# RWKV-7 stage of a four-mixer decoder trunk: key blocks first, state in two half-head chains, outputs and LayerNorm with dims on partitions

## The chip, the cores and the metric

One core of a Trainium2 chip runs the whole kernel. The metric is the device time of one execution in microseconds, as the median of several runs.

## The reference, cut to what matters

Four layers, each `h = h + Mixer(RMSNorm(h))` and `h = h + SqReLU_MLP(RMSNorm(h))`, on x of (1, 256, 1024) float32; the mixers are S5, mLSTM, FoX and RWKV-7 in that order. The change touches RWKV-7 alone (16 heads of 64):

```python
xr, xw, xk, xv, xa, xg = (x + dx * mu[idx] for idx in range(6))   # dx = x_prev - x
r, k, v = xr @ W_r, xk @ W_k, xv @ W_v
w_log = -softplus(-(w0 + tanh(xw @ W_w) @ w_up)) - 0.5;  decay = exp(-exp(w_log))
a = sigmoid(a0 + (xa @ W_a) @ a_up);  g = sigmoid(xg @ W_g) @ g_up
kk = heads(k * k_k), normed per head;  k_mod = k * (1 + (a - 1) * k_a)
def step(state, inp):
    sa = einsum('bhij,bhj->bhi', state, -kk_t)
    state = state * w_t + sa (x) (kk_t * a_t) + v_t (x) k_t      # (x): outer product
    return state, einsum('bhij,bhj->bhi', state, r_t)
y = head_layer_norm(y) * ln_g + ln_b + sum(r * k_mod * r_k) * v
out = (y * g) @ w_out
```

## The kernel before, in words

The stages run one after another: s5, mlp0, mlstm, mlp1, fox, mlp2, rwkv, mlp3, final. Activations of the RWKV stage are kept turned, with 128 of the 1024 dims on partitions and the 256 time steps in columns, as eight tiles, taken in four blocks b of two tiles (four heads). Half hf is blocks 2hf and 2hf+1. The recurrence is taken in four chunks c of 64 steps: within a chunk it is a triangular system, between chunks a state of 64x64 per head is carried.

- *Head* (L1383 to L1402): the reciprocal norm of each row is spread over partitions by a matmul (`rstd_row`, L372), h is transposed, and VectorE scales it (xn, L1392). `mix` (L1402) is eight VectorE multiply-adds that make one of the six mixed inputs into one of the two halves of xm.
- *main* (L1792): the small projections wl and al, then for each b `k_part` and `r_part`, then `v_part` for each b, then gl. A block's projection (`projN`, L422) is 16 float32 matmuls, 32 instructions, into one of two PSUM banks with the tag pa; weights come through SyncE's queue into three buffers w.
- *k_part* (L1427): pw and pq (L1436, L1437), tanh, the scan of the decay over a chunk (L1448), exponentials, then after k the squares, and in `rest` pn (L1480: the block matrix bones times the squares), Ln and Exp (L1483, L1484) and five VectorE steps (L1486 to L1491) into X and bk. Its temporaries hold the tags s, hi, lo, two buffers each; `rest` ends with the last use of hi and lo.
- *inner* (L1541), one per half: products of bk (weights) and X, both its a half (64 columns) and its r half (64 columns) in one matmul of 128 columns (L1553), masks, a regrouping through memory (L1578, L1581: ScalarE's queue writes, then reads), a 15-step loop on VectorE (L1599, L1601), a second round trip (L1605, L1608), and the block solve z, dx, dy (L1634 to L1666). The PSUM banks are acc0 to acc3.
- *over* (L1674): the four chunks one behind another, both halves together: b1, rh, b3, sv, b4, scaled state, and the outputs in b2 (L1686 to L1716), with time steps on partitions. `norm` (L1720) takes bn_stats per head, a Pool power, and 8 ScalarE scalings a chunk (L1734).
- *gate* (L1742): the gate's projection (L1752, L1753). *outp* (L1758): transposes py (L1768), 8 ScalarE scalings by ln_g and ln_b (L1776), two VectorE steps, the split in two fp32r parts, then the output projection: each of the eight weight blocks times both parts, 12 matmuls of 512 columns (L442; in `tail` L474).

Order: these are generators, run by `Order` (L143). It takes the next name of a hand-written list (`SEQ["rwkv"]`, L211) that can go; with the list used up, of the tasks whose inputs are ready by `Clock`'s own costs the one with the lowest priority number (the third argument of `spawn`), then the oldest. A task waits at `yield event`; `od.fire` sets an event. What is written earlier has priority; on an engine a later instruction can stand ahead of an earlier one that has to wait for operands or buffers.

Of the kernel before, what the change touches and what calls it, by code (L numbers as in the profile page):

```python
# [8 lines left out]
F32 = mybir.dt.float32  # L9
# [9 lines left out]
KT = 8  # L19
# [123 lines left out]
class Order:  # L143
# [22 lines left out]
    def run(self):  # L166
# [44 lines left out]
    "rwkv": (  # L211
# [1140 lines left out]
def rwkv(K):  # L1352
# [9 lines left out]
    with ExitStack() as st:  # L1362
# [22 lines left out]
        rb = K.rstd_row(K.rstd())  # L1385
        for kp in range(KT // 2):
            if kp % 2 == 0:
                xts = K.turned(kp // 2)
            p = xts[kp % 2]
            n, k0 = kp // 2, 2 * (kp % 2)  # L1390
            for j in range(2):
                nc.vector.scalar_tensor_tensor(out=xn[n][:, k0 + j], in0=p[:, j * T:(j + 1) * T],  # L1392
                                               scalar=col("rw_norm_g", 2 * kp + j), in1=rb, op0=ALU.mult, op1=ALU.mult)
            x = xn[n][:, k0:k0 + 2]
            nc.scalar.mul(dx[n][:, k0:k0 + 2, :1], x[:, :, :1], -1.0)
            nc.vector.tensor_tensor(out=dx[n][:, k0:k0 + 2, 1:], in0=x[:, :, :T - 1], in1=x[:, :, 1:], op=ALU.subtract)
        xm = K.xtp.tile([128, 2, KT, T], F32, name="xm", tag="xhl")

        def mix(n, dst):

            for k in range(KT):
                nc.vector.scalar_tensor_tensor(out=xm[:, dst, k], in0=dx[k // 4][:, k % 4], scalar=col("rw_mu", n * KT + k),  # L1402
                                               in1=xn[k // 4][:, k % 4], op0=ALU.mult, op1=ALU.add)
            return xm[:, dst]

# [9 lines left out]
        ready = [Event(), Event()]  # L1415
        v_ev = [Event() for _ in range(4)]
        t_ev, f_ev = [Event(), Event()], Event()
        y_ev = Event()
        g_ev = Event()
        yn, rbm, Yt = [None] * 2, [None] * 2, [None] * 2  # L1420
        C = -0.5 * float(np.exp(-0.5))
        tmp, kks = {}, []
        q4 = lambda n, t, bufs=2: one.tile(SHAPE4, F32, name=n, tag=t, bufs=bufs)
        bank = lambda n, k: K.pacc.tile([128, 512], F32, name=n, tag=f"acc{k}")
        u3 = lambda t: t.rearrange("p a c t -> p (a c) t")

        def k_part(b, xk):  # L1427
# [22 lines left out]
            E1 = dbl.tile([128, 2, 4, 65], F32, name="E1", tag="E1")  # L1450
# [6 lines left out]
            yield GO  # L1457
            out = []
            yield from K.projN(two(i["rw_k"], b), xk, out)
            pk = out[0]  # L1460
# [16 lines left out]
            def rest():  # L1477
# [10 lines left out]
                for e in range(2):  # L1488
                    nc.vector.scalar_tensor_tensor(out=X[hf][R[e], e, ps0, :, :64], in0=kr[R[e]], scalar=-1.0,
                                                   in1=E1[R[e], :, :, :64], op0=ALU.mult, op1=ALU.mult)  # L1490
                    nc.vector.scalar_tensor_tensor(out=bk[b][R[e], :, :, e], in0=tha[R[e]], scalar=0.5, in1=E2[R[e]],  # L1491
                                                   op0=ALU.mult, op1=ALU.mult)
                yield GO
            tmp["kk", b] = od.spawn(f"k{b}", rest())
            kks.append(tmp["kk", b])

        def r_part(b, xr):
# [11 lines left out]
            if b % 2:  # L1509
                od.fire(ready[hf])  # L1510
# [29 lines left out]

        def inner(hf):  # L1541

            yield ready[hf]
            for ev in kks[2 * hf:2 * hf + 2]:
                yield ev
            x = X[hf]
            ar = q4("araw", "ar")
            rb_ = rbm[hf] = q4("rb", "rb")
            for p in range(4):
                ms = [bank(f"m{hf}", 2 * (p % 2) + e).rearrange("p (c t) -> p c t", c=4) for e in range(2)]  # L1550
                for c in range(4):
                    for e in range(2):
                        nc.tensor.matmul(ms[e][:, c], bk[2 * hf + p // 2][R[e], p % 2, c].rearrange("p a t -> p (a t)"),  # L1553
                                         x[R[e], e, p, c], start=True, stop=True)
                for e in range(2):
                    m = ms[e]
                    kr, br = R[1 - e], R[e]
                    nc.scalar.copy(out=ar[br, p], in_=m[br, :, :64])
                    nc.vector.tensor_tensor(out=x[kr, e, p], in0=m[kr], in1=mask[kr].unsqueeze(1).broadcast_to([64, 4, 128]),
                                            op=ALU.mult)  # L1560
                    nc.scalar.copy(out=rb_[br, p], in_=m[br, :, 64:])
                yield WAIT if p % 2 else GO
            for e in range(2):
                nc.gpsimd.affine_select(out=u3(rb_)[R[e]], in_=u3(rb_)[R[e]], pattern=[[0, 16], [1, 64]],
                                        compare_op=ALU.is_ge, fill=0.0, base=0, channel_multiplier=-1)
# [16 lines left out]

            for b in (2 * hf, 2 * hf + 1):
                bkT[b] = one.tile([128, 2, 2, 4, 64], F32, name="bkT", tag="bk", bufs=5)
                for p in range(2):
                    t = bank(f"bt{hf}", 2 * hf + p).rearrange("p (c e t) -> p c e t", c=4, e=2)
                    for c in range(4):
                        nc.tensor.transpose(t[:, c].rearrange("p e t -> p (e t)"),
                                            bk[b][:, p, c].rearrange("p a t -> p (a t)"), K.ident)
                    nc.scalar.copy(out=bkT[b][:, :, p].rearrange("p e c t -> p c e t"), in_=t)  # L1590
                    yield GO
# [36 lines left out]
            for g in range(2):  # L1628
                us = slice(8 * g, 8 * g + 8)
                au = aus[g]  # L1630
                z = bank(f"z{hf}", 2 * hf).rearrange("p (u t) -> p u t", u=8)
# [6 lines left out]
                dx_ = bank(f"dx{hf}", 2 * hf + 1).rearrange("p (u t) -> p u t", u=8)  # L1638
                dy = bank(f"dy{hf}", 2 * hf).rearrange("p (u t) -> p u t", u=8)
# [11 lines left out]
            z = bank(f"z2{hf}", 2 * hf).rearrange("p (u t) -> p u t", u=16)  # L1651
# [10 lines left out]
            dy = bank(f"dy2{hf}", 2 * hf + 1).rearrange("p (u t) -> p u t", u=16)  # L1662
# [11 lines left out]
        def over():  # L1674

            for ev in t_ev + v_ev:
                yield ev
            pairs = [(hf, p, e) for hf in range(2) for p in range(4) for e in range(2)]
            for hf in range(2):
                yn[hf] = q4("yn", "ar")  # L1680
            sc = None
            bk8 = lambda n, k: bank(n, k).rearrange("p (a b) -> p a b", a=8)
            for c in range(4):
                b1, b2 = bk8("b1", 0), bk8("b2", 2 + c % 2)
                for hf, p, e in pairs:
                    nc.tensor.matmul(b1[R[e], 4 * hf + p], X[hf][:, e, p, c, :64], sv[:, hf, e, p, c], start=True, stop=True)  # L1686
                rh = K.ev.tile([128, 8, 64], F32, name="rh", tag="lo")
                nc.scalar.copy(out=rh, in_=b1)
                for hf, p, e in pairs:
                    nc.tensor.matmul(b2[R[e], 4 * hf + p], X[hf][:, e, p, c, 64:], sv[:, hf, e, p, c], start=(hf + p == 0), stop=False)  # L1690
                yield WAIT
                b3 = bk8("b3", 1)
                for hf, p, e in pairs:
                    nc.tensor.matmul(b3[R[e], 4 * hf + p], Yt[hf][R[e], p, c], rh[R[e], 4 * hf + p], start=True, stop=True)
                s8 = lambda e, c: sv[R[e], :, e, :, c, :]
                b8 = lambda t: t.rearrange("p (h a) t -> p h a t", h=2)
                nc.scalar.copy(out=s8(0, c), in_=b8(b3[R[0]]))
                nc.vector.tensor_copy(out=s8(1, c), in_=b8(b3[R[1]]))
                yield WAIT
                if c < 3:  # L1700
                    b4 = bk8("b4", 0)
                    for hf, p, e in pairs:
                        nc.tensor.matmul(b4[R[e], 4 * hf + p], bkT[2 * hf + p // 2][:, e, p % 2, c], sv[:, hf, e, p, c], start=True, stop=True)
                    eb = eL[:, :, c].unsqueeze(2).broadcast_to([128, 8, 64])
                    sn = K.ev.tile([128, 8, 64], F32, name="sc", tag="s")
                    src = b4
                    if sc is not None:
                        nc.vector.tensor_tensor(out=sc, in0=sc, in1=b4, op=ALU.add)
                        src = sc
                    for e in range(2):  # L1710
                        nc.vector.tensor_tensor(out=s8(e, c + 1), in0=b8(src[R[e]]), in1=b8(eb[R[e]]), op=ALU.mult)
                    if c < 2:
                        nc.vector.tensor_tensor(out=sn, in0=src, in1=eb, op=ALU.mult)
# [289 lines left out]
```

## Time and profile before

| | us |
|---|---|
| median of 3 runs (lowest to highest) | 1406.84 (1398.44 to 1409.97) |
| profiled execution | 1410.3 |
| its span, first to last instruction | 1408.6 |
| TensorE busy / VectorE / ScalarE | 1323.0 / 873.0 / 716.1 |
| mean granted TensorE clock | 0.966 |

The profile lists each instruction of one execution. A matmul's row lasts until its modelled end, which overlaps the next one's, so what one costs in a stream is the distance from start to start. A busy share near 100% at a clock below 1 is not full work: the granted clock says how fast TensorE was allowed to run. PE is TensorE's matmuls, PEld its weight loads, DVE VectorE, ACT ScalarE, ACTq ScalarE's DMA issue.

### The profile page before, as it was taken

How to read it: one execution, taken by the hardware profiler on the slowest of the kernel's cores; microseconds unless marked ns; L12 is line 12 of the kernel's file. 1: busy time of each engine (PE TensorE's matmuls, PEld its weight loads, DVE VectorE, ACT ScalarE, POOL GpSimd, SP SyncE). 2: the span in 40 equal slices, each digit the busy share in tenths (PEclk: the TensorE clock that was granted, in tenths of full speed). 3: DMA queues.
4: the chain of work that ended last, by engine and by line, in shares of the span. 5: the costliest groups of instructions: out<-in, count | busy, mean ns of one | idle time of the engine just before them, and what ended most of it. 6: DMA issues, size and time to landing. Idle time of an engine off the chain costs nothing.

```text
span 1408.6 us, 23397 instructions
## 1 busy us (share of the span) xinstructions
PE 1323.0 (94%) x9492; PEld 1155.8 (82%) x9492; DVE 873.0 (62%) x1431; ACT 716.1 (51%) x1188; POOL 41.8 (3%) x64
## 2 busy tenths in 40 slices
PE   4799999999999999999999999998998888899997
PEld 3667989998988999889888999986777675799996
DVE  8985555568786555575866555556686443555554
ACT  7945454457645544464554644442544346454443
POOL 3000000001010000000100000000000010000000
PEclk9699999999999999999999999999999996899998
DMA  4045555564535655556334555552333211355553
GB/s 176 16 132 181 166 184 192 183 200 157 184 131 166 193 183 191 187 168 245 123 119 163 181 193 182 192 183 78 117 113 96 78 51 44 113 191 191 190 184 120
DMA packets 71532, 216.14 MB, mean 153 GB/s; under 512 B 19132, under 2 KB 19732, under 8 KB 70912
## 3 DMA queue, kind: packets, MB, share of 16 engines
q1 hardware_dynamic: 56880, 206.30, 44.5%
q10 hardware_dynamic: 14496, 8.24, 2.1%
q8 instruction: 74, 1.21, 0.4%
q14 instruction: 34, 0.28, 0.1%
q0 software_dynamic: 48, 0.11, 0.0%
HBM read 211.71 MB, written 2.91 MB: 152 GB/s over the span
## 4 chain that ended last, share of the span: by engine, by line
PE 60%; issue 18%; DVE 12%; DMA 5%; ACT 4%; POOL 1%; ACTq 0%; POOLq 0%; SPq 0%; DVEq 0%
PE acc L442 21%; PE pa L383 8%; PE pa L384 8%; PE pa L385 8%; PE pa L422 5%; DVE wl L288 2%; PE g L442 1%; ACT wh L287 1%; PE acc L474 1%; PE pa L406 1%; PE pa L408 1%; DVE pd L1599 1%; PE pa L407 1%; DMA w<-in_fox_qk 1%; DVE t L627 1%
## 5 line engine op out<-in xcount | busy, mean ns | idle before, releaser
L288 DVE TENSOR_TENSOR wl<-w,wh 128x1024 fp32r<-128x1024 f32 x350 | 430.4, 1231 | 374.1 <-ACT wh L287 373.3
L287 ACT ACTIVATE wh<-w 128x1024 fp32r<-128x1024 f32 x350 | 370.3, 1059 | 448.0 <-PE pa L384 148.4
L385 PE MATMUL pa<-xhl,wl 128*128 128x256 f32 x1264 | 358.1, 283 | 2.0 <-DVE wl L288 2.0
L383 PE MATMUL pa<-xhl,wh 128*128 128x256 f32 x1264 | 359.4, 284 | 0.0
L384 PE MATMUL pa<-xhl,wh 128*128 128x256 f32 x1264 | 358.1, 283 | 0.0
L383 PEld LDWEIGHTS pa<-xhl,wh 128*128 128x128 f32 x1264 | 242.1, 192 | 4.5 <-issue 1.2
L384 PEld LDWEIGHTS pa<-xhl,wh 128*128 128x128 f32 x1264 | 242.2, 192 | 2.9 <-issue 0.5
L385 PEld LDWEIGHTS pa<-xhl,wl 128*128 128x128 f32 x1264 | 242.2, 192 | 2.6 <-DVE wl L288 2.6
L442 PE MATMUL acc<-wh,hi 128*128 128x512 f32 x552 | 172.8, 394 | 2.6 <-ACT hi L287 1.8
L442 PE MATMUL acc<-wl,hi 128*128 128x512 f32 x552 | 171.4, 392 | 0.0
L442 PE MATMUL acc<-wh,lo 128*128 128x512 f32 x552 | 170.9, 391 | 0.1
L442 PEld LDWEIGHTS acc<-wl,hi 128*128 128x128 f32 x552 | 104.2, 189 | 22.6
L442 PEld LDWEIGHTS acc<-wh,lo 128*128 128x128 f32 x552 | 104.1, 189 | 22.7 <-DVE lo L288 0.5
L422 PE MATMUL pa<-xm,w 128*128 128x256 f32 x448 | 112.2, 403 | 4.8 <-DVE xm L1402 4.8
L442 PEld LDWEIGHTS acc<-wh,hi 128*128 128x128 f32 x552 | 99.6, 190 | 20.6 <-ACT hi L287 2.1
L422 PEld LDWEIGHTS pa<-xm,w 128*128 128x128 f32 x448 | 86.3, 200 | 21.0 <-DVE xm L1402 5.5
L288 DVE TENSOR_TENSOR lo<-s,hi 128x512 fp32r<-128x512 f32 x64 | 43.9, 685 | 1.4 <-ACT hi L287 1.4
L507 DVE SCALAR_TENSOR_TENSOR s<-pa,r 128x512 f32<-128x512 f32 x64 | 43.8, 684 | 0.0
L287 ACT ACTIVATE hi<-s 128x512 fp32r<-128x512 f32 x64 | 39.5, 617 | 5.3 <-DVE s L507 5.3
L505 ACT ACTIVATE r<-pa 128x512 f32<-128x512 f32 x64 | 37.1, 580 | 0.0
L442 PE MATMUL acc<-wh,xhl 128*128 128x512 f32 x128 | 34.9, 391 | 0.0
L353 ACT ACTIVATE xhl<-xt,vecs 128x256 fp32r<-128x256 f32 x48 | 21.0, 472 | 22.4 <-PE xt L338 20.3
(392 smaller groups left out, 1572.2 us busy)
## 6 DMA issues: line engine op xcount, KB each, us to landing
w<-in_mlp_up SPq DMA_DIRECT2D x128, 512.0 KB, 3.5
w<-in_mlp_dn SPq DMA_DIRECT2D x128, 512.0 KB, 3.5
w<-in_s_w_glu SPq DMA_DIRECT2D x16, 512.0 KB, 4.2
w<-in_fox_qk SPq DMA_DIRECT2D x16, 512.0 KB, 4.0
w<-in_ml_qk SPq DMA_DIRECT2D x8, 512.0 KB, 3.8
w<-in_ml_v SPq DMA_DIRECT2D x8, 512.0 KB, 3.5
w<-in_ml_o SPq DMA_DIRECT2D x8, 512.0 KB, 3.4
w<-in_ml_out SPq DMA_DIRECT2D x8, 512.0 KB, 3.4
```

The costliest lines, as they stand in the source:

```text
L287: self.nc.scalar.activation(out=hi, in_=src, func=AF.Copy)
L288: self.nc.vector.tensor_tensor(out=lo, in0=src, in1=hi.bitcast(F32), op=ALU.subtract)
L353: nc.scalar.activation(out=xhl[:, k, 0, :], in_=s, func=AF.Identity, scale=g)
L383: nc.tensor.matmul(out, wh[:, ks], xhl[:, k, 0, :], start=(k == 0), stop=False)
L384: nc.tensor.matmul(out, wh[:, ks], xhl[:, k, 1, :], start=False, stop=False)
L385: nc.tensor.matmul(out, wl[:, ks], xhl[:, k, 0, :], start=False, stop=(k == KT - 1))
L406: nc.tensor.matmul(o, wh[:, ks], xhl[:, k, 0, :], start=(k == 0 and f == 0), stop=False)
L407: nc.tensor.matmul(o, wh[:, ks], xhl[:, k, 1, :], start=False, stop=False)
L422: nc.tensor.matmul(p[:, f * T:(f + 1) * T], w[:, k * 128:(k + 1) * 128], x[:, k], start=(k == 0), stop=(k == KT - 1))
L442: nc.tensor.matmul(acc[tt * 2 + n], a[:, ts], w[:, n * 512:(n + 1) * 512], start=s0, stop=s1)
L505: nc.scalar.activation(out=r, in_=p, func=AF.Relu)
L507: nc.vector.scalar_tensor_tensor(out=s, in0=p, scalar=0.0, in1=r, op0=ALU.max, op1=ALU.mult)
```

## The change

The list `SEQ["rwkv"]` is taken out, so the order comes from priorities and `Clock`. Rows of h are scaled by the reciprocal norm before they are transposed, and the first mix is made pair by pair. `main` runs k0 to k3, then r0 to r3, then v0 to v3, then gl; the second gate weights come on SyncE's queue into w buffers. `inner` starts on kks and multiplies X's first half; `rmul` does X's second half after r. `over` and `norm` run once per half; the output matmul has its operands exchanged, so that y has dims on partitions in banks acc1 and acc3 (half 0) or pa (half 1). LayerNorm is two matmuls with block matrices (cen takes off the mean, bones sums the squares), Ln and Exp; ln_g and ln_b are folded into the gate and into bv.

```diff
+        rr = K.rstd()
+        hn = [[K.ev.tile([128, 512], F32, name="hn", tag=("r", "hi")[n]) for tt in range(2)] for n in range(2)]
+            nc.scalar.activation(out=hn[n][0], in_=K.h[0][:, hs], func=AF.Copy, scale=rr[:, 0:1])
+            nc.vector.tensor_scalar(out=hn[n][1], in0=K.h[1][:, hs], scalar1=rr[:, 1:2], scalar2=None, op0=ALU.mult)
...
+                nc.scalar.activation(out=xn[n][:, k0 + j], in_=p[:, j * T:(j + 1) * T], func=AF.Copy,
+                                     scale=col("rw_norm_g", 2 * kp + j))
...
+            mix(1, 0, (2 * kp, 2 * kp + 1))
...
+        def products(b, ms, ts):
+            for p in range(2):
+                for c in range(4):
+                    for e in range(2):
+                        nc.tensor.matmul(ms[e][:, p, c], bk[b][R[e], p, c].rearrange("p a t -> p (a t)"),
+                                         x[R[e], e, p0 + p, c, ts], start=True, stop=True)
+            for e in range(2):
+                nc.vector.tensor_tensor(out=x[kr, e, p0:p0 + 2, :, ts], in0=ms[e][kr],
...
+        def rmul(b):
+            yield r_ev[b]
+            yield kks[b]
+            ms = products(b, [K.ps("mr", "ps") for e in range(2)], slice(64, 128))
...
         def inner(hf):
-            yield ready[hf]
+            for b in (2 * hf, 2 * hf + 1):
+                yield kks[b]
+                ms = products(b, [bank(f"m{hf}", 2 * (b % 2) + e) for e in range(2)], slice(0, 64))
...
-                dx_ = bank(f"dx{hf}", 2 * hf + 1).rearrange("p (u t) -> p u t", u=8)
-                dy = bank(f"dy{hf}", 2 * hf).rearrange("p (u t) -> p u t", u=8)
+                dx_ = bank(f"dx{hf}", 3).rearrange("p (u t) -> p u t", u=8)
+                dy = bank(f"dy{hf}", 2).rearrange("p (u t) -> p u t", u=8)
...
-        def over():
-            for ev in t_ev + v_ev:
+        def over(hf):
+            for ev in (t_ev[hf], *v_ev[2 * hf:2 * hf + 2], *rms[2 * hf:2 * hf + 2]):
                 yield ev
+            if hf:
+                yield g_ev
+            w = bank(f"ov{hf}", 2 * hf).rearrange("p (g a t) -> p g a t", g=2, a=4)
+                yp[2 * hf + j] = K.pp.tile([128, 512], F32, name="pa", tag="pa", bufs=2) if hf else bank("y", 1 + 2 * j)
...
+                    nc.tensor.matmul(y4[p // 2][R[e], p % 2, c], sv[:, hf, e, p, c], X[hf][:, e, p, c, 64:],
+                                     start=(c == 0 and p % 2 == 0), stop=False)
...
+        def norm(hf):
+            yield gate_ev
+            if hf:
+                yield n_ev[0]
+            for b in bs:
+                nc.scalar.copy(out=yb, in_=yp[b])
+                nc.tensor.matmul(pc[b], cen, yb, start=True, stop=True)
+                nc.scalar.activation(out=sq[b], in_=pc[b], func=AF.Square, scale=0.125)
+            for b in bs:
+                nc.tensor.matmul(pv, bones, sq[b], start=True, stop=True)
+                nc.scalar.activation(out=rs[b], in_=pv, func=AF.Ln, bias=eps)
+            for b in bs:
+                nc.scalar.activation(out=rs[b], in_=rs[b], func=AF.Exp, scale=-0.5)
+            for b in bs:
+                nc.vector.tensor_tensor(out=u, in0=pc[b], in1=rs[b], op=ALU.mult)
+                nc.vector.tensor_tensor(out=u, in0=u, in1=gates[b].rearrange("p a t -> p (a t)"), op=ALU.mult)
+                nc.vector.tensor_tensor(out=u, in0=u, in1=bv[b].rearrange("p a t -> p (a t)"), op=ALU.add)
+                od.fire(u_ev[b])
...
         def outp(b):
-            yield y_ev
-            yield gate_ev
+            yield u_ev[b]
...
         def main():
+            yield from K.projN(two(i["rw_k"], 0), xk, out)
+            for b in range(4):
+                k_part(b, out[b])
+                yield GO
+                if b < 3:
+                    yield from K.projN(two(i["rw_k"], b + 1), xk, out)
+                    yield kks[b]
+            for b in range(4):
                 yield from r_part(b, xr)
...
+            for n in range(2):
+                gup.append(K.wraw.tile([128, D], F32, name="w", tag="w"))
+                nc.sync.dma_start(out=gup[n][:rows], in_=i["rw_g_up"][128 * n:128 * n + rows])
...
+        rms = [od.spawn(f"r{b}", rmul(b), 1) for b in range(4)]
+        for hf in range(2):
+            od.spawn(f"c{hf}", over(hf), 0)
```

## Rows read from the trace of the kernel before

**Rows 1.** Busy time by stretch of the RWKV stage, in us.

```profile
core 0: us, PE busy (x) PEld busy (x) DVE busy (x) ACT busy (x) POOL busy (x), PEclk, DMA share, GB/s
949.00:970.40 21.40, 14.45 (x62) 10.88 (x60) 18.65 (x48) 3.36 (x13) 2.07 (x5) 0.84 0.13 36
970.40:1058.00 87.60, 85.86 (x444) 69.91 (x444) 61.18 (x126) 41.61 (x82) 2.52 (x4) 0.98 0.36 117
1058.00:1126.00 68.00, 57.99 (x823) 45.95 (x823) 34.50 (x68) 28.78 (x60) 2.93 (x4) 0.90 0.34 90
1126.00:1162.40 36.40, 31.81 (x637) 25.54 (x633) 18.33 (x73) 15.59 (x41) 4.92 (x3) 1.00 0.17 51
1162.40:1181.70 19.30, 14.59 (x34) 7.25 (x33) 3.52 (x21) 10.61 (x26) 1.64 (x1) 0.50 0.00 0
1200.30:1217.30 17.00, 10.30 (x40) 7.98 (x38) 6.87 (x11) 7.30 (x14) 0.00 (x0) 0.70 0.18 63
```

**Rows 2.** TensorE in order of time: start, us, operation, count, idle before.

```profile
958.95 9.92 PE L422 MATMUL pa<-xm,w 128*128 128x256 f32 x32 [4.80 <-DVE xm L1402]
...
970.38 14.08 PE L422 MATMUL pa<-xm,w 128*128 128x256 f32 x64
984.30 1.02 PE L1480 MATMUL pn<-sq,cst 128*128 128x512 f32 x2
...
1005.41 1.13 PE L1437 MATMUL pq<-tw,up 64*128 64x256 f32 x4
1006.47 1.13 PE L422 MATMUL pa<-xm,w 128*128 128x256 f32 x4
1007.53 1.16 PE L1553 MATMUL m<-X,bk 64*128 64x128 f32 x16
1008.62 1.13 PE L422 MATMUL pa<-xm,w 128*128 128x256 f32 x4
...
1129.93 1.15 PE L1694 MATMUL b<-rh,Y 64*64 64x64 f32 x32
...
1139.97 0.70 PE L422 MATMUL pa<-xm,w 128*128 128x256 f32 x2
...
1199.38 0.62 PE L442 MATMUL acc<-wl,hi 128*128 128x512 f32 x2
1199.84 0.62 PE L442 MATMUL acc<-wh,lo 128*128 128x512 f32 x2
```

**Rows 3.** Groups by line and form, 948 to 1217 us, TensorE and ScalarE.

```profile
L422 PE MATMUL pa<-xm,w 128*128 128x256 f32 x448 | 112.2, 403 | 4.8 <-DVE xm L1402 4.8
L1553 PE MATMUL m<-X,bk 64*128 64x128 f32 x128 | 10.5, 290 | 4.2 <-ACT rb L1561 4.2
L1776 ACT ACTIVATE y<-py,vecs 64x128 f32<-64x128 f32 x32 | 14.5, 454 | 0.9 <-PE py L1768 0.5
```

**Rows 4.** VectorE and ScalarE in order of time: mixes, then the key chain.

```profile
959.41 12.35 DVE L1402 SCALAR_TENSOR_TENSOR xm<-dx,vecs,xn 128x256 f32<-128x256 f32 x31
...
995.54 1.27 DVE L1448 TENSOR_TENSOR_SCAN L<-reset,ld 128x256 f32<-128x256 f32 x2
...
1004.51 1.28 ACT L1483 ACT_TABLE_LOAD   x1
...
1005.81 0.63 ACT L1483 ACTIVATE rn<-rn 128x512 f32<-128x512 f32 x1
...
1008.77 0.69 DVE L1486 TENSOR_TENSOR kr<-kr,rn 128x512 f32<-128x512 f32 x1 [3.82 <-ACT rn L1484]
...
1014.07 1.25 DVE L1448 TENSOR_TENSOR_SCAN L<-reset,ld 128x256 f32<-128x256 f32 x2
...
1039.35 1.26 DVE L1448 TENSOR_TENSOR_SCAN L<-reset,ld 128x256 f32<-128x256 f32 x2
```

**Rows 5.** The chain of waits, 1056 to 1084 us: start, us, what.

```profile
1058.80 5.18 DMA rw_y<-yx
```

**Rows 6.** Transfers of the page: KB of one, us from issue to landing.

```profile
w<-in_mlp_dn SPq DMA_DIRECT2D x128, 512.0 KB, 3.5
```

More of the change, by code (lines that the diff above doesn't have):

```diff
@@ L1384, in rwkv, with mix @@
         dx = [K.whl.tile([128, 4, T], F32, name=f"dx{n}", tag="wl") for n in range(2)]
[L1385 to L1396, printed above, removed]
         xm = K.xtp.tile([128, 2, KT, T], F32, name="xm", tag="xhl")
-        def mix(n, dst):
-            for k in range(KT):
+        def mix(n, dst, ks=range(KT)):
+            for k in ks:
                 nc.vector.scalar_tensor_tensor(out=xm[:, dst, k], in0=dx[k // 4][:, k % 4], scalar=col("rw_mu", n * KT + k),
@@ L1681, in over @@
             sc = None
-            bk8 = lambda n, k: bank(n, k).rearrange("p (a b) -> p a b", a=8)
             for c in range(4):
[L1684 to L1687, printed above, removed]
+                b1, b3 = w[:, 0], w[:, 1]
+                for p, e in pairs:
+                    nc.tensor.matmul(b1[R[e], p], X[hf][:, e, p, c, :64], sv[:, hf, e, p, c], start=True, stop=True)
@@ L1693, in over @@
[L1693 to L1698, printed above, removed]
+                for p, e in pairs:
+                    nc.tensor.matmul(b3[R[e], p], Yt[hf][R[e], p, c], rh[R[e], p], start=True, stop=True)
@@ L1699, in over @@
+                nc.scalar.copy(out=s4(0, c), in_=b3[R[0]])
+                nc.vector.tensor_copy(out=s4(1, c), in_=b3[R[1]])
                 yield WAIT
                 if c < 3:
[L1701 to L1705, printed above, removed]
@@ L1706, in over @@
-                    src = b4
+                    for p, e in pairs:
+                        nc.tensor.matmul(b1[R[e], p], bkT[2 * hf + p // 2][:, e, p % 2, c], sv[:, hf, e, p, c], start=True, stop=True)
+                    eb = eL[:, 4 * hf:4 * hf + 4, c].unsqueeze(2).broadcast_to([128, 4, 64])
+                    src = b1
                     if sc is not None:
-                        nc.vector.tensor_tensor(out=sc, in0=sc, in1=b4, op=ALU.add)
+                        nc.vector.tensor_tensor(out=sc, in0=sc, in1=b1, op=ALU.add)
@@ L1717, in over @@
[L1717 removed]
+                for p, e in pairs:
+                    nc.tensor.matmul(y4[p // 2][R[e], p % 2, c], sv[R[e], hf, e, p, c], rbm[hf][R[e], p, c],
+                                     start=False, stop=(c == 3 and p % 2 == 1))
                 yield WAIT
[L1720 to L1737 removed]
@@ new lines, in gate @@
+                    nc.tensor.matmul(pg[:, js], gup[0][:, fs], sg[0], start=True, stop=False)
+                    nc.tensor.matmul(pg[:, js], gup[1][:32, fs], sg[1], start=False, stop=True)
+                for j in range(2):
+                    js = slice(j * T, (j + 1) * T)
+                    nc.scalar.activation(out=gates[b][:, j], in_=pg[:, js], func=AF.Copy, scale=col("rw_ln_g", 2 * b + j))
+                    nc.vector.scalar_tensor_tensor(out=bv[b][:, j], in0=bv[b][:, j], scalar=col("rw_ln_b", 2 * b + j),
+                                                   in1=pg[:, js], op0=ALU.add, op1=ALU.mult)
```

199 lines of the change are left out of this document (90 added, 109 removed), and 5 rows, old and new, of the table SEQ.

## The prediction

> **What bounds the kernel now.** I read the time by stretch first, then TensorE in order of time, then the groups by form, and last the chain of one key block. The reader should see in the stretches [rows 1] that the RWKV stage, from 949.0 us (the transposes of its input) to 1217.3 us (the first matmul of the last MLP), takes 268.3 us, and that TensorE is near full only in one part of it: 85.9 of 87.6 us at a granted clock of 0.98 from 970.4 to 1058. Elsewhere it is idle or at the lower of its two levels (1.2 of 2.4 GHz): clock 0.84 in the head, 0.90 and 10.0 us idle from 1058 to 1126, then the serial state chain (36.4 us), then 19.3 us at 0.50 with the gate and the first output block, then 17.0 us at 0.70 at the end. So the question is how much of the stage is matmul work and how much is loss, and what the change does to each.
>
> **Work and loss before.** One matmul instruction costs, from start to next start at the full level [rows 2]: a projection (984.30 - 970.38) / 64 = 0.2175 us; pq 1.06 / 4 = 0.265; a product of bk and X 1.09 / 16 = 0.068; one of the 64-column kind 1.15 / 32 = 0.036; a 512-column one of the block sums 1.02 / 2 = 0.5; one of the output projection 0.46 / 2 = 0.23. The counts are in [rows 3] (projections 448, products 128) or in the code. The last projection ends at 1140.7 [rows 2], which cuts the stage in three:
> - Head, 949.0 to 970.4: 21.4 us.
> - Middle, 970.4 to 1140.7: 170.3 us. Work: 416 projections 90.5, pw and pq 6.4, pn and pb 8.0, products 8.7, the block solve's 384 at 0.036 = 13.8, 256 of the state chain 9.2, transposes and 32-wide ones about 11 (my estimate, the same on both sides): 147.6. Loss 22.7.
> - Tail, 1140.7 to 1217.3: 76.6 us. Work: 352 of the state chain 12.7, gate 32 x 0.265 = 8.5, output projection 96 x 0.23 = 22.1, transposes 4: 47.3. Loss 29.3.
>
> **The change, part by part.**
>
> *Head.* The rstd row and its multiply go; two ScalarE and two VectorE scalings come in front of the transposes, xn is then a ScalarE copy, and the first mix runs inside the loop over pairs. Before, TensorE idles 4.80 us ahead of the first projection and then goes at VectorE's pace, 31 mixes in 12.35 us, 0.40 each [rows 2, 4]. VectorE now has 8 multiplies of 0.40 fewer and 4 small columns and 2 scalings more: about 2 us less. I let the first key block be done at 971.7, in place of about 977.4 (970.4 plus 32 x 0.2175). But the pw and pq of that block (8 x 0.265 = 2.1), done before 970.4 until now, come after it. Head with first key block: 22.7 us. Net -3.6 (bounds 0 and -6, the idle time and the 2 us).
>
> *Key blocks first.* k0 to k3 run without the r blocks between them; each k_part starts when the one before has fired kks. The chain of one block, scan, exponentials, square, pn, Ln, Exp, five products, is serial through the buffers hi and lo. Scans stand at 995.54, 1014.07 and 1039.35: 18.5 and 25.3 us apart [rows 4], with TensorE queues and other blocks between. The 18.5 us of block 1 are 10.3 from the scan to Ln at 1005.81, 3.0 to the first product at 1008.77 and 5.3 to the next scan. The first part holds waits for TensorE, whose queue had r's projections in front of pn; I cut it to 7, my estimate, and take 15 a block. A block gives TensorE only 16 x 2 x 0.2175 = 7.0 plus 3.1 for pw, pq and pn, 10 us. pa has two banks, so TensorE can be two blocks ahead: it has about 31 us of work up to the moment when k2's bank comes free for r0, at about 2 x 15 + 6.5 = 36.5 us. Loss 5, and 4 more while r0 and r1 share one bank. I take 9 (bounds 0 and 30, the latter with 25.3 a block). This work was done between r blocks before, at no loss.
>
> A page of the Trainium skill speaks against this part: "ScalarE: Activation LUTs", section "What ACT_TABLE_LOAD costs", puts a switch of tables at 1283 ns and a drain of 1380 ns behind it. By that a block's two switches would add 2.8 us, three blocks 8 us. The trace has the load at 1004.51 and the next function at 1005.81 [rows 4], 1.30 us later, with no drain between; the sum goes by the row.
>
> *Products in two passes.* r no longer has to be there: X's first 64 columns are multiplied in inner, the last 64 in rmul. So bk is loaded as weights twice, 256 instructions of half the moving columns. If the load of 128 columns sets the pace, as the 0.068 for 128 moving columns suggests beside 0.036 for 64-column weights, each still costs 0.068: 17.4 in place of 8.7, +8.7 on TensorE, on the path, since it is the bound there. Bounds 0 (half the columns, half the time) and +8.7.
>
> The skill's page "TensorE: Matmul & The Clock Gate", section "LDWEIGHTS (loading the stationary operand)", gives columns / 1.2 ns, 107 ns for 128 columns whatever the rows. By it the second pass would add 128 x 0.107, an estimate of 13.7 us. The row has 0.068 for load and matmul together [rows 2], so the measurement decides for the lower figure.
>
> *The solve of the triangles starts earlier.* inner(0) no longer waits for r1, inner(1) not for r3 but for the last kks, some 971 + 4 x 15 = 1031. What follows it is about 55 us by my estimate (two round trips through memory at about 10, the 15-step loop 9, the block solve 13, masks and waits for the rest), so it ends near 1090, with projections still to run for 50 us. That removes most of the idle time of 1058 to 1126. What stays: ScalarE's queue stands while it waits to issue the second transfer of a round trip, 5.18 us at the longest [rows 5]; four of these, two now inside the key chain. Middle loss besides the key blocks: 7 in place of 22.7 (bounds 3 and 20).
>
> *State in two chains.* Half 0 runs under the v blocks, half 1 after the gate's inputs. The instructions stay 608, at half the width for VectorE and ScalarE. The chain of both halves takes 36.4 / 4 = 9.1 us a chunk [rows 1]; half the width gives between 4.6 and 9.1, I take 6.5, 26 us for half 1, and beside it stand the gate, the norm of half 0 and the first output blocks, 8.5 + 4 + up to 11, so TensorE is nearly covered. SyncE's queue now carries the gate's weights: they hold two of the three w buffers until the gate is done, so that w_out has one till then. A load lands in 3.5 us [rows 6] and with its split takes some 6; the first output block is due some 20 us after the last projection, time for three, so I cost this at nothing (6 us if the gate comes late). Pool's masks for r (8 halves in place of 4) stand beside everything else: Pool is busy 2.9 of 68 us [rows 1].
>
> *Outputs with dims on partitions.* The 64 scalings of ScalarE go: 32 of y take 14.5 us, 454 ns each [rows 3], and they stand in the 19.3 and the 17.0 us stretch. So do bn_stats, four Pool powers and py. In come 16 matmuls of 512 columns, 16 x 0.5 = 8 us on TensorE, and ScalarE's copies, squares, Ln and Exp. For half 1 this is a chain of about 11 us behind the state; out-projection 0 and 1 (11 us) can cover it.
>
> **The sum.** Middle after: 384 projections 83.5, pw and pq 8.5, pn and pb 8.0, products 17.4, solve 13.8, half 0's state 304 x 0.036 = 10.9, rest 11: 153.1, plus 9 and 7 of loss: 169.1. Tail after: state 10.9, gate 8.5, norm 8, projection 22.1, transposes 2: 51.5, plus 6 of loss (bounds 2 and 25, the latter if the clock falls as it does after 1162.4): 57.5. With the head's 22.7: 249.3 against 268.3, 19.0 us less. The work rises by about 9 us; what is gained is loss in the tail and the middle. The profiled execution took 1410.3 us (span 1408.6): 1391.3. The median of the runs shown, 1406.84, is 3.5 below it: 1388. The other stages are not touched.
>
> **Rivals.**
> - *A: the key chain stays at the 25 us a block that it shows at its worst.* For it: two of the round trips' 5 us stands now fall into it, and table loads lie in it. Against: before, TensorE's queue and the r blocks stretched it. It adds 20 us or so to the middle: 1406, no change.
> - *B: slower. Bank 3 is held.* over(0) accumulates its outputs in banks 1 and 3 and they are released only by norm(0), which comes after the gate; inner(1) needs bank 3 for dx and dy. If over(0) takes it first, inner(1)'s rest (13 us), the state of half 1 (26), its norm (11) and output blocks stand one behind another after norm(0) at about 18 us behind the last projection, with TensorE at the lower level as in the 0.50 stretch: 1135 + 18 + 13 + 26 + 11 + 13 and 8 for the clock is 1224, 7 us later than before: 1414. It decides when inner(1) is not through its last dx before v1 is done, about 1085; my figure for inner(1) is 1090, so it is close. Against: only if the written order lets half 0 in front, and a key chain of 15 us brings inner(1) forward.
> - *C: the losses are half of mine.* Buffers let r blocks and over(0) fill every gap: key loss 4, middle 3, tail 3: 1376.
> - That the edits don't take effect is not a case here: each is a visible change of instructions.
>
> **How the numbers follow.** Forecast 0.50 (own range 1378 to 1402), A 0.18, B 0.14, C 0.18. A measurement of this kernel can tell about 1%, 14 us: faster by more is below 1392.8. Of the forecast 0.36 lies there, with C 0.54; within 1%: 0.14 of the forecast, 0.14 of A, 0.04 of B, 0.32; slower: the worse ends of A and B, 0.14. The range 1362 to 1414 takes in C's better end and B's centre.
>
> **What would show it.** Right: gaps in TensorE between k0 and r0 of 5 to 15 us in all; the last projection near 1141; products at 0.068 in both passes; from the last projection to the next MLP under 60 us. Wrong: scans of the key blocks over 20 us apart; dx of inner(1) behind norm(0); a tail at clock 0.5 to its end; product passes at 0.034.

## The result: 1.1% slower, and the profile after

| | before | after |
|---|---|---|
| median of 4 runs (us) | 1407.49 | 1421.39 (1419.54 to 1423.71) |
| ratio, 95% interval | 1 | 1.0111 [1.0063, 1.0160] |
| RWKV stage of the profiled execution | 268.3 | 278.5 |

The medians lie 13.9 us apart; the ratio, which is one of means, puts the loss between 9 and 22.5 us.

The stage in the changed kernel, by stretch (columns as in [rows 1]; head with the first key block, two parts of the middle with the key blocks, the rest of the middle, then two parts of the tail):

```profile
948.30:971.00 22.70, 18.15 (x82) 14.65 (x80) 17.83 (x48) 6.35 (x16) 2.85 (x8) 0.92 0.22 77
971.00:1000.00 29.00, 26.91 (x129) 19.77 (x128) 14.67 (x23) 17.87 (x34) 0.00 (x0) 0.90 0.28 91
1000.00:1044.00 44.00, 38.23 (x141) 28.03 (x141) 26.85 (x57) 18.76 (x34) 0.00 (x0) 0.66 0.19 55
1044.00:1162.30 118.30, 114.87 (x1413) 94.09 (x1411) 55.82 (x122) 35.17 (x71) 6.42 (x10) 0.95 0.26 76
1162.30:1193.90 31.60, 28.16 (x330) 18.40 (x329) 16.89 (x32) 16.07 (x29) 0.00 (x0) 0.92 0.31 101
1193.90:1226.80 32.90, 29.73 (x133) 21.34 (x131) 17.36 (x24) 20.09 (x26) 0.00 (x0) 0.97 0.30 96
```

The middle takes 191.3 us where 169.1 were forecast. Its damage is above all the 44 us at a clock of 0.66, where before the same time ran at 0.98 [rows 1]. From 971 to 1044 TensorE is idle for 7.9 us, and the clocks of 0.90 and 0.66 take some 18 more: about 26 us lost, an estimate from the two rows, where 9 were allowed. TensorE in order of time shows how it got there (L416 is L422 of before, L1552 the products, L1485 pn):

```profile
989.05 2.00 PE L1552 MATMUL m<-X,bk 64*128 64x64 f32 x32
993.14 0.70 PE L416 MATMUL pa<-xm,w 128*128 128x256 f32 x2 [2.09 <-DVE km L1477]
993.68 1.38 PE L1485 MATMUL pn<-sq,cst 128*128 128x512 f32 x2
994.99 2.07 PE L1445 MATMUL pw<-tw,up 64*128 64x256 f32 x4
...
998.14 2.07 PE L1446 MATMUL pq<-tw,up 64*128 64x256 f32 x4
```

After 2.09 us without a matmul, pw and pq take 2.07 us each, where pq took 1.13 before [rows 2]: the lower level. VectorE at the same time, with the scans that mark the key blocks:

```profile
973.56 1.27 DVE L1457 TENSOR_TENSOR_SCAN L<-reset,ld 128x256 f32<-128x256 f32 x2
988.27 1.27 DVE L1457 TENSOR_TENSOR_SCAN L<-reset,ld 128x256 f32<-128x256 f32 x2
991.08 1.41 DVE L1556 TENSOR_TENSOR X<-m,cst 64x512 f32<-64x512 f32 x2 [1.54 <-PE m L1552]
992.42 0.67 DVE L1477 TENSOR_TENSOR km<-km,pa 128x512 f32<-128x512 f32 x1
...
1005.58 0.48 DVE L1384 SCALAR_TENSOR_TENSOR xm<-dx,vecs,xn 128x256 f32<-128x256 f32 x1 [9.75 <-PE pa L416]
1006.01 0.69 DVE L1491 TENSOR_TENSOR kr<-kr,rn 128x512 f32<-128x512 f32 x1
...
1011.65 1.27 DVE L1457 TENSOR_TENSOR_SCAN L<-reset,ld 128x256 f32<-128x256 f32 x2
...
1033.93 0.69 DVE L1457 TENSOR_TENSOR_SCAN L<-reset,ld 128x256 f32<-128x256 f32 x1
```

The reader should see a ring: TensorE waits for km, km stands behind the mask of the products (991.08), and that waits for TensorE. The first period is 14.7 us, the next two are 23.4 and 22.3. A mix for the v blocks also waits 9.75 us in front of kr.

### The profile page after: what moved, and what is told of

Same layout as the page of the kernel before. It is cut to its first block, busy times and chain, and to the rows that moved or that the text cites. A ratio compares the mean times of both kernels' runs of the same rounds, so it can differ in the third digit from the quotient of the medians.

```text
span 1417.8 us, 23579 instructions
## 1 busy us (share of the span) xinstructions
PE 1345.2 (95%) x9616; PEld 1169.3 (82%) x9616; DVE 868.9 (61%) x1382; ACT 711.6 (50%) x1147; POOL 36.7 (3%) x65
## 4 chain that ended last, share of the span: by engine, by line
PE 79%; DVE 9%; DMA 5%; ACT 5%; issue 2%; ACTq 0%; POOLq 0%; POOL 0%; SPq 0%; DVEq 0%
PE acc L436 27%; PE pa L377 10%; PE pa L378 10%; PE pa L379 10%; PE pa L416 7%; DVE wl L282 2%; PE acc L468 1%; ACT wh L281 1%; PE pa L400 1%; PE pa L402 1%; PE pa L401 1%; PE g L436 1%; PE m L1552 1%; DMA w<-in_fox_qk 1%; PE xt L332 1%
## 5 line engine op out<-in xcount | busy, mean ns | idle before, releaser
L416 PE MATMUL pa<-xm,w 128*128 128x256 f32 x448 | 119.6, 418 | 8.5 <-DVE km L1477 7.5
L436 PEld LDWEIGHTS acc<-wh,lo 128*128 128x128 f32 x552 | 103.6, 188 | 23.4 <-DVE lo L282 0.9
L416 PEld LDWEIGHTS pa<-xm,w 128*128 128x128 f32 x448 | 89.3, 208 | 28.3 <-DVE km L1477 8.6
L297 ACT ACTIVATE junk<-h 128x512 f32<-128x512 f32 x36 | 22.5, 624 | 17.1 <-DVE h L451 16.4
```

What stands on the lines that cost most here:

```text
L297: self.nc.scalar.activation(out=junk, in_=self.h[tt][:, n * 512:(n + 1) * 512], func=AF.Square, accum_out=self.sq[:, n, tt:tt + 1])
L416: nc.tensor.matmul(p[:, f * T:(f + 1) * T], w[:, k * 128:(k + 1) * 128], x[:, k], start=(k == 0), stop=(k == KT - 1))
L436: nc.tensor.matmul(acc[tt * 2 + n], a[:, ts], w[:, n * 512:(n + 1) * 512], start=s0, stop=s1)
```

## The experiments

Theories: **T**, TensorE starves on key blocks alone, drops to its lower level, and the chain, which runs through TensorE, slows with it; **Q**, waits in VectorE's queue, above all that of the mix for v; **L**, the lost hand-written order; later **G**, the products of the two partition halves standing apart. Ratios, and distances in us, are to the kernel before in runs beside each; the change as it stands is 13.9 us above it (1421.39 less 1407.49), and the distances of two kernels are compared. Where the intervals of two kernels overlap, the difference of their distances is not clear of noise; that holds for the head alone against run 4, for all of run 6 against its parent, for the copy's gains in run 7, and for holding the mix back in run 8.

**1. r blocks between the key blocks again.**

```diff
-            for b in range(4):
-                yield from r_part(b, xr)
+                yield from r_part(b, xr)        # in the key loop, behind the projection of k(b+1)
```

> The changed kernel, but each r block projected again between the key blocks (k0, k1, r0, k2, r1, k3, r2, r3). Theory T (with only key blocks to do, TensorE waits for the chain of one block, falls to its lower level, and the chain itself then slows): the granted clock stays near 1.0 from 971 to 1044, the last projection comes at about 1143 instead of 1162, and the time is about 1400 to 1405 us. Rival L (it is the missing hand-written order of the stage that costs): 1415 to 1422 us, with the idle time somewhere else. Rival Q (the waits that stand in VectorE's queue in front of the key chain, above all the mix for v): at most 5 us better, 1416 us.

1415.52 us, 1.0034 [1.0012, 1.0056]: 5.8 us above before, so 8 back, not 20. T's range was missed; the figure lies at the lower end of L's and half a microsecond under Q's bound, so it doesn't part those two. The order is a part only, and the clock still dips (0.83 from 1000 to 1030). The mix for v moved with the r blocks, into the last round of the loop.

**2. The mix for v issued later.**

```diff
-            xv = mix(3, 0)
             for b in range(4):
                 yield from r_part(b, xr)
+                if b == 1:
+                    xv = mix(3, 0)
```

> The changed kernel, but the mix for v is issued after the second r block, not ahead of the first. Q: VectorE no longer stands 9.75 us in front of the products of key block 1, so the third scan comes 4 to 8 us earlier (about 1005 instead of 1011.65), and the time is 1411 to 1417 us. T: the gap in TensorE at 991 and the low clock behind it stay, so at most 4 us better, 1417 to 1421 us.

1421.09 us, 1.0081 [1.0049, 1.0112]: 11.4 above. The trace shows the mix still waiting 9.47 us in front of kr: the planner put it back, so this run said nothing of Q.

**3. Matmuls in the gaps.**

```diff
+        def fill(n):
+            f = bank("fill", n)
+            for k in range(8):
+                nc.tensor.matmul(f[:, :T], K.ident, xm[:, 1, k], start=True, stop=True)
```

> The changed kernel with 24 idle-time matmuls of 256 columns (8 before the last key block, 8 before each of the first two r blocks) whose results nobody reads: 24 x 0.44 = 10.5 us of TensorE work more, at full level. T: the clock stays at 1.0 from 990 to 1044, the scans stand 15 to 18 us apart, and in spite of the added work the time is equal or better, 1405 to 1420 us. Rival (the chain of a key block takes 23 us whatever TensorE's level is): the fillers sit in part in the gaps, 3 to 10 us slower, 1424 to 1431 us.

Eight stand before the last key block and eight before each of the first two r blocks.

1410.70 us, 1.0006 [0.9993, 1.0019]: 1.0 above, 13 us faster than the change with more work. TensorE, as above (L1815 is the added work), then VectorE:

```profile
989.71 2.00 PE L1552 MATMUL m<-X,bk 64*128 64x64 f32 x32
991.64 2.86 PE L1815 MATMUL fill<-xm,ident 128*128 128x256 f32 x12
994.34 1.02 PE L1485 MATMUL pn<-sq,cst 128*128 128x512 f32 x2
995.29 1.13 PE L1445 MATMUL pw<-tw,up 64*128 64x256 f32 x4
...
998.57 6.21 PE L416 MATMUL pa<-xm,w 128*128 128x256 f32 x28
1004.71 3.17 PE L1552 MATMUL m<-X,bk 64*128 64x64 f32 x32
...
1022.55 2.00 PE L1552 MATMUL m<-X,bk 64*128 64x64 f32 x16
1024.48 0.70 PE L416 MATMUL pa<-xm,w 128*128 128x256 f32 x2
```

```profile
988.93 1.27 DVE L1457 TENSOR_TENSOR_SCAN L<-reset,ld 128x256 f32<-128x256 f32 x2
...
1005.85 1.27 DVE L1457 TENSOR_TENSOR_SCAN L<-reset,ld 128x256 f32<-128x256 f32 x2
1007.70 1.41 DVE L1556 TENSOR_TENSOR X<-m,cst 64x512 f32<-64x512 f32 x2 [0.21 <-PE m L1552]
```

pn starts 5.4 us after the scan, as in the change, but pw takes 1.13 us, and the scans stand 16.9 us apart. T's signs came in part: the clock is 1.00 from 971 to 1000 but 0.92 from 1000 to 1044, and the third period is 19.5 us. But the planner had also put kr in front of the mix here, and the third scan in front of the mask, so T and Q weren't apart yet; run 8 takes that up.

**4. The kernel before without its list.** Only `SEQ["rwkv"]` goes.

> The kernel before with nothing but the hand-written order of this stage taken out, so that the planner orders it. L: 1418 us or more, i.e. the list was worth as much as the change lost. T: the list is worth little by itself, 1403 to 1413 us, because the r blocks still stand between the key blocks.

1398.02 us, 0.9925 [0.9902, 0.9949]: L is dead, with the opposite sign, and T's 1403 to 1413 was missed too. The list alone was a cost of 11.7 us: without it the stage takes 257.6 us. Its last stretches by time, and the state chain's first matmuls:

```profile
971.00:1136.60 165.60, 152.60 (x1572) 124.28 (x1571) 101.44 (x214) 73.81 (x149) 8.07 (x9) 0.94 0.34 103
1136.60:1202.50 65.90, 51.82 (x444) 39.01 (x443) 30.17 (x88) 37.83 (x83) 4.91 (x3) 0.87 0.19 59
```

```profile
1119.09 1.15 PE L1680 MATMUL b<-sv,X 128*64 128x64 f32 x32
...
1135.92 0.70 PE L416 MATMUL pa<-xm,w 128*128 128x256 f32 x2
...
1153.48 0.70 PE L1746 MATMUL pg<-sg,gup 128*128 128x256 f32 x2
```

In the kernel before, the gate's matmuls behind the chain:

```profile
1162.38 1.22 PE L1752 MATMUL pg<-sg,gup 128*128 128x256 f32 x2
```

The state chain starts 17 us ahead of the last projection (before: 14, at 1125.77), and it ends at 1153.5, 17 us behind that projection's end (before: 22, at 1162.4). The gate's matmuls that follow it go at the full level, where before they went at the lower. Together that is a tail of 65.9 us where before had 76.6. So from here each other part of the change is set against 1398 us.

**5. Three parts of the change, each put into the kernel of run 4, and what is left without two of them.** Key blocks first (the r loop behind the key loop, four E1 buffers):

> The kernel before without the hand-written order (1398 us), and with the four key blocks ahead of the four r blocks (four E1 buffers for it). T (key blocks alone starve TensorE and its level falls): the scans stand over 20 us apart from the second on, the granted clock is under 0.8 for some 40 us, and the time is 1405 to 1415 us. Rival (the order does no harm by itself, only together with the split products): 1395 to 1402 us.

1410.15 us, 1.0012 [0.9992, 1.0031]: +12.8 us. The clock was 0.83 from 1000 to 1030, and the scans 18.0, 13.8 and 18.4 us apart: the price as T had it, its signs in part. Behind 2.42 us without a matmul pn and pw take 1.77 and 2.07 us, the lower level, but no period is over 20 us and the clock isn't under 0.8 for 40 us.

Products in two passes in one place:

```diff
-                        nc.tensor.matmul(ms[e][:, c], ..., x[R[e], e, p, c], start=True, stop=True)
+                for ts in (slice(0, 64), slice(64, 128)):
...
+                            nc.tensor.matmul(ms[e][:, c, ts], ..., x[R[e], e, p, c, ts], start=True, stop=True)
```

> The kernel before without the hand-written order (1398 us), and with each product of bk and X as two matmuls of 64 columns, all of the first halves and then all of the second of a pair of heads. If the load of the weights sets the pace, 256 matmuls at 0.0625 us add 8 us of TensorE, where it is the bound: 1402 to 1407 us. Rival (they fall into gaps): 1396 to 1400 us.

1403.91 us, 0.9967 [0.9952, 0.9983]: +6.6 us, in the range of the first expectation. The head alone:

> The kernel before without the hand-written order (1398 us), and with the changed head alone (rows scaled, then transposed, the first mix in the loop). The head ends about 3 us earlier: 1392 to 1396 us. Rival (the planner's order changes and the gain is given back at the next wait): 1396 to 1401 us.

1395.20 us, 0.9902 [0.9878, 0.9926]: -2.1 us, as expected. The changed kernel with r between and products in one pass (run 1 with the inner loop of before):

> The changed kernel with the r blocks between the key blocks (1415.5 us as measured) and with the products again in one pass of 128 columns, issued when r is there. What is left of the change is the head, the two half-head chains and the outputs with dims on partitions. If the second pass costs what its rows show (8 us): 1405 to 1409 us. If it is hidden: 1412 to 1417 us. If it comes below 1398 us, the rest of the change is a gain by itself; above it, a loss.

1397.81 us, 0.9929 [0.9908, 0.9951]. Against the head alone, the two half-head chains and the new outputs together are no gain (+2.6 us, intervals overlapping). And run 1 differs from this one only by what belongs to the separate passes: 17 us. That takes in the earlier start of the solve, since here `inner` waits for r again.

**6. The tail, and the second pass in one place** (all from 1397.81 us). Gate weights in the bk buffers; one Exp for both blocks of a half; both; and the split of the products as in run 5.

```diff
-                gup.append(K.wraw.tile([128, D], F32, name="w", tag="w"))
+                gup.append(one.tile([128, D], F32, name="gup", tag="bk", bufs=5))
...
-            for b in bs:
-                nc.scalar.activation(out=rs[b], in_=rs[b], func=AF.Exp, scale=-0.5)
+            nc.scalar.activation(out=rs2, in_=rs2, func=AF.Exp, scale=-0.5)
```

> The kernel with the r blocks between and the products in one pass (1397.8 us), and the gate's weights in the bk buffers, so that all three w buffers are there for the output projection. If the bunched splits of w_out behind the norm of half 1 set the end of the tail (2.28 us of idle TensorE at hi, 0.34 at wl): 2 to 4 us better, 1394 to 1396 us. If the norm of half 1 sets it: no change, 1396 to 1399 us.

1400.41 us, 0.9946 [0.9925, 0.9966]: +3.4 us, above both expectations; the w buffers weren't the limit.

> The same kernel (1397.8 us) with the two Exp of a half's norm as one instruction over both blocks, so that Ln, Ln, Exp needs two table loads and not four: two loads of 1.28 us go from the chain behind half 1's state, 2 to 3 us better, 1395 to 1396 us. If the splits of w_out end later than that chain: no change.

1394.97 us, 0.9918 [0.9880, 0.9955]: -2.0 us, about as expected, though less than the interval's width; its tail is 59.7 us, that of its parent 63.2. ScalarE's table loads for half 1, in the changed kernel and then here:

```profile
1203.12 1.28 ACT L1762 ACT_TABLE_LOAD   x1 [0.99 <-PE pn L1760]
1204.42 0.69 ACT L1762 ACTIVATE rs<-pn,eps 128x512 f32<-128x512 f32 x1
1205.13 1.28 ACT L1765 ACT_TABLE_LOAD   x1
1206.42 0.63 ACT L1765 ACTIVATE rs<-rs 128x512 f32<-128x512 f32 x1
1207.07 1.28 ACT L1762 ACT_TABLE_LOAD   x1
...
1209.07 1.28 ACT L1765 ACT_TABLE_LOAD   x1
```

```profile
1178.52 1.28 ACT L1753 ACT_TABLE_LOAD   x1
...
1181.68 1.28 ACT L1755 ACT_TABLE_LOAD   x1
1182.97 1.06 ACT L1755 ACTIVATE rs<-rs 128x1024 f32<-128x1024 f32 x1
```

> Both edits of the tail together (from 1397.8 us). If they stand in one chain behind each other: 4 to 6 us better, 1392 to 1394 us, which is below the best so far (1395.2 us). If one hides the other: 1394 to 1396 us.

1398.70 us, 0.9932 [0.9915, 0.9949]: +1.7 us, the two don't add, and both expectations were missed.

> The same kernel (1397.8 us) with each product as two matmuls of 64 columns, both issued when r is there, in the same place. The second pass by its price alone (128 x 0.0625 = 8 us of TensorE, of which 6 showed in the kernel before): 1403 to 1406 us. If the 17 us between this kernel and the one with a separate second pass were all its price: 1412 us or more; what is missing to 1415 us is then the placement (the first halves multiplied while the key chain runs, second halves through the banks of pw, pq and pn).

1400.07 us, 0.9939 [0.9918, 0.9960]: +3.1 us, under both expectations. So of the 17 us between run 1 and its one-pass sibling, the second pass itself is the smaller part.

**7. The products' halves side by side.** In the trace of run 3, 16 rows of one partition half take 2.00 us (1022.55; that half's mask starts at 1024.59, ahead of the other 16 rows) at the full level (a projection behind them goes at 0.70 for two rows), while 32 alternating rows take 2.00 us (989.71). G: a small copy that makes both halves ready at once restores the alternation.

```diff
+                t = bk[b][:, :, :, 0, 0:1]
+                nc.vector.tensor_copy(out=t, in_=t)
                 od.fire(kks[b])
```

Added to run 1:

> The changed kernel with the r blocks between the key blocks (1415.5 us), and one small VectorE copy (8 columns of bk onto themselves, on all 128 partitions) behind the last write of a key block, so that the products of both halves of the partitions become ready at once and are issued in turn. Theory G (the products of one half, issued one after another, take 0.125 us each, in turn 0.0625): the first pass falls from 17.9 us of busy time to about 10, and the time to 1405 to 1411 us. Rival (the separate second pass costs by the queues and the lower level): 1413 to 1418 us.

1409.66 us, 1.0015 [0.9993, 1.0038]: -5.3 us by one tiny instruction a block and in G's range. The groups of products, in run 1 and then here (busy us, mean ns):

```profile
L1552 PE MATMUL m<-X,bk 64*128 64x64 f32 x128 | 17.9, 317 | 0.7 <-DVE bk L1496 0.7
```

```profile
L1554 PE MATMUL m<-X,bk 64*128 64x64 f32 x128 | 12.5, 304 | 1.9 <-DVE bk L1499 1.9
```

The second pass's group, mr, rose from 13.0 to 14.9 us, so both passes together fell by 3.5.

Added to the changed kernel, to the best version so far, and to run 3:

> The changed kernel with that small copy alone. G: three of its four blocks had their first-pass products by halves; 3 us less of busy time, but in part in the stretch where TensorE waits for the key chain: 1417 to 1421 us. T and G together would leave the rest to the low level.

1415.85 us, 1.0057 [1.0024, 1.0090]: -7.2 us, more than expected.

> The kernel with the r blocks between, the products in one pass, the joint Exp of the norm (1395.0 us), and the small copy. G: products 14.0 us busy before, 11 at the most now: 1391 to 1395 us; if nothing is left to gain there, 1394 to 1397 us.

1394.54 us, 0.9905 [0.9880, 0.9931]: within the interval of the head alone.

> The changed kernel with the idle-time matmuls (1410.7 us) and the small copy: key blocks first and products in two passes kept. T and G together: the level stays at full and the first-pass products go in turn: 1406 to 1410 us. If it stays at 1410 to 1413 us, grouping costs nothing once the level is kept.

1409.88 us, 1.0004 [0.9979, 1.0030]: nothing beyond the fillers' gain, and a third key block whose 32 rows go in turn:

```profile
1021.90 2.00 PE L1554 MATMUL m<-X,bk 64*128 64x64 f32 x32
```

**8. The mix really held back**, its factors made to pass through the first r block's output, without fillers.

```diff
+                    nc.vector.scalar_tensor_tensor(out=mu3, in0=prod[0][:, 0, 0, :8], scalar=0.0, in1=mu, ...)
```

> The changed kernel with the mix for v made to depend on the evacuation of the first r block (its factors pass through a small multiply-add with that block's output), so that it can't stand in front of the key chain in VectorE's queue; no idle-time matmuls. Q (that wait is what stretched the chain, and the idle-time matmuls helped by moving it): the second to third scan falls from 23.4 us to 17 to 19, and the time is 1409 to 1414 us. T (the lower level of TensorE stretched it): the gaps of TensorE at km and the level under 0.8 stay, at most 4 us better, 1416 to 1420 us.

1422.34 us, 1.0101 [1.0072, 1.0131], outside both ranges (T: 1416 to 1420). Q falls as far as the mix goes: kr follows ScalarE at once, and still the scans are 23.0 us apart.

```profile
992.03 1.27 DVE L1457 TENSOR_TENSOR_SCAN L<-reset,ld 128x256 f32<-128x256 f32 x2
...
1006.14 0.69 DVE L1491 TENSOR_TENSOR kr<-kr,rn 128x512 f32<-128x512 f32 x1 [6.12 <-ACT rn L1489]
1014.29 0.69 DVE L1556 TENSOR_TENSOR X<-m,cst 64x512 f32<-64x512 f32 x1 [4.00 <-PE m L1552]
1015.02 1.27 DVE L1457 TENSOR_TENSOR_SCAN L<-reset,ld 128x256 f32<-128x256 f32 x2
```

```profile
997.44 1.85 PE L1485 MATMUL pn<-sq,cst 128*128 128x512 f32 x2
...
1004.38 7.95 PE L416 MATMUL pa<-xm,w 128*128 128x256 f32 x28
1012.26 3.39 PE L1552 MATMUL m<-X,bk 64*128 64x64 f32 x32
```

Now the mask stands in front of the scan and waits for products, which TensorE reaches 20.2 us after the scan; in run 3, with more matmul rows in between, it reaches them after 15.8 (988.93 to 1004.71). pn starts 5.4 us after the scan in both, so these 4.4 us a block are the lower level's. They reach the scan only because the mask stands in front of it in VectorE's queue; in run 3 the scan stands first. With the small copy as well:

> The same with the small copy that restores the alternation of the products (with it the changed kernel took 1415.9 us, with copy and idle-time matmuls 1409.9 us). Q: 1408 to 1411 us, as with the idle-time matmuls, though TensorE idles. T: 1412 to 1416 us, and a level under 0.8 in the key blocks.

1410.23 us, 1.0016 [0.9991, 1.0041]: T's figure missed, Q's met. Without the copy, holding the mix back brought nothing; with it, 4.6 us. The copy's own gain here, 12.1 us, is clear of noise. The trace shows what else the copy did:

```profile
991.25 1.27 DVE L1457 TENSOR_TENSOR_SCAN L<-reset,ld 128x256 f32<-128x256 f32 x2
...
1010.09 1.27 DVE L1457 TENSOR_TENSOR_SCAN L<-reset,ld 128x256 f32<-128x256 f32 x2
1014.60 1.41 DVE L1558 TENSOR_TENSOR X<-m,cst 64x512 f32<-64x512 f32 x2 [3.24 <-PE m L1554]
```

```profile
997.06 1.91 PE L1485 MATMUL pn<-sq,cst 128*128 128x512 f32 x2
...
1012.56 2.00 PE L1554 MATMUL m<-X,bk 64*128 64x64 f32 x32
```

TensorE is again at the lower level and reaches the products 21.3 us after the scan, but the next scan now stands in front of the mask, and the scans are 18.8 us apart. So of the 6.1 us between the periods of 23.0 and 16.9, 1.9 are the lower level in the chain itself (18.8 against run 3) and 4.2 the mask in front of the scan. These are single executions: this one took 1423.44 us, 13 above its median, and that of the run without the copy 1428.58. The copy changes the alternation too; no run changes the order alone.

## Why the prediction was wrong, point by point

- **The step that failed is "Key blocks first": 15 us a block and a loss of 9.** The first period was 14.7, the next ones 23.4 and 22.3, and some 26 us went from 971 to 1044. I sized the chain with TensorE at its full level, let a gap cost its own length, and listed only the chain's own steps, with no wait in VectorE's queue between them. With the gaps filled and the copy (the last kernel of run 7) the second period is 15.1 us (989.91 to 1005.02) and the third 17.1. The level that falls behind each gap delays pn, pw, pq, the next projection and the products (4.4 us a block by the time the products start); what reaches the next scan of this is 1.9 us with the scan in front of the mask, and 6.1 with the mask in front (run 8). In the change the mix for v stands in front of kr besides. Filling the gaps brought 13 us in spite of 10.4 us of added work (48 rows at 0.2175): that run's middle, 971.7 to 1151.4, is 179.7, or 169.3 without the fillers, against 169.1 forecast. That the two agree so closely is luck: its periods were 16.9 and 19.5 us, not 15. Rival A named the slow period, but let it cost 20 us only.
- **Products in two passes** were priced at 8.7; the rows at 32 in 2.00 us bear that out, and +6.6 and +3.1 us came of it in one place. Not seen: the first pass, issued early, puts its masks into the key chain and lets the halves fall apart. The earlier start of the solve, which the first pass was split off for, brought nothing that shows: the kernel of 1397.81 us gives up both.
- **Head**: done at 971.0, forecast 971.7; alone worth 2.1 us.
- **The other loss of the middle**, 7 in the sum: 3.4 us of idle time and a clock of 0.95 over the 118.3 us behind 1044, some 9.
- **Tail**: 64.5 us, forecast 57.5. The four table loads of half 1's norm in place of two are 2.6 of it; TensorE also waits 2.79 us for sv, behind the norm of half 0 in VectorE's queue. The Trainium skill ("ScalarE: Activation LUTs", "What ACT_TABLE_LOAD costs") adds a drain of 1380 ns to a switch; the rows have the next function 1.30 us after a load's start, so here a load alone.
- **What the tail's gain was credited to**: 29.3 us of loss before were to fall by the two chains and the new outputs. Taking the list out gives 10.7 of that with the old code. Rival B didn't occur: dx of inner(1) ran from 1102 to 1109, the state of half 0 from 1127. Of the prediction's signs of being wrong, only the scans over 20 us apart came.
- **A misreading that changes little**: 0.036 and 0.5 us for the matmuls of 64 and 512 columns are lengths of rows; from start to start the rows have 0.034 (1129.93 to 1131.01) and 0.475 (984.30 to 985.25).

In sum, by the distances: list out -11.7, head -2.1, chains and outputs +2.6, second pass +3.1, first pass apart, with the solve's earlier start, +14.0, key blocks first +8.1, which makes the 13.9. The parts depend on what they are added to: key blocks first cost 12.8 in run 5. The +8.1 is near the 9 allowed for, but the first pass, priced at its 8.7 alone, falls into the same stretch, and its masks are part of what the key chain waits for there. The remedies (fillers; copy with r between; copy with the mix held) all end within 2.1 us of before and don't add. What of the +14.0 is left behind the copy's 5.3 stays open: that the masks stand in the scan's way is read from traces with both orders (run 8), not tried by itself. The two kernels that beat both are the head alone without the list (0.9902) and the one with r between, one pass, joint Exp and copy (0.9905); they tie, and neither is clear of taking the list out alone (0.9925): the intervals overlap.

## What to carry to other kernels

When work that fills an engine is moved away from a chain that runs through it, ask what level the engine will run at in the gaps, and price the chain at that level. Then look what stands in front of the chain's next step in each queue: an instruction that waits for the slowed engine passes the whole delay on. Before crediting a rewrite, run the old code without its hand-written order: here that deletion was worth more than any part of the rewrite. An experiment that reorders the source must be read back from the trace, since the planner may undo it.

## What was unexpected of the hardware

Products on partitions 0 to 63 and on 64 to 127 cost 0.0625 us each when they alternate and 0.125 when one half's stand together, at the same level. The Trainium skill ("TensorE: Matmul & The Clock Gate", "Part 3: Packing small matmuls — row/col tiling") says that a weight load overlaps a matmul in flight only if its row group differs; the rows agree, and the price of losing it is a factor of two.

Behind the same wait of 2.09 us for km the level fell in the change and in both runs of 8 (pn then takes 1.38, 1.85 and 1.91 us) and stayed in the profiled execution of the changed kernel with the copy (run 7, 1.02 us). That kernel's ten executions reach from 1407.31 us at a mean clock of 0.980 to 1426.30 us at 0.962.
